# A batched matrix product: one of eight output groups stored in six strided transfers

## The chip, the cores and the metric

The kernel runs on one core of a Trainium2 chip. The metric is the device time of one execution in microseconds, as the median of several runs.

## The reference

```python
batch, dim_i, dim_j, dim_k = 32, 256, 512, 384
x: (32, 256, 512) float32,  y: (32, 512, 384) float32

def reference(x, y):
    return np.einsum('bij,bjk->bik', x, y).astype(np.float32)
```

Thirty-two independent products of a 256 x 512 matrix with a 512 x 384 matrix, read and written in float32: 16.8 MB of x, 25.2 MB of y and 12.6 MB of output.

## The kernel before

**Tiling.** The 32 batches are worked in N = 8 groups of Q = 4. In a group each batch has PQ = 32 of the 128 partitions. For x and for the output a partition holds R = 8 consecutive rows of its batch, for y T = 16 consecutive rows. So in memory each partition's share of a group is one contiguous run: 16 KB of x, 24 KB of y, 12 KB of output. The output run falls into two halves of 6 KB, one for each half `e` (NE = 2; H = 4 rows of 384 floats).

**Engines.** SyncE (SP) issues all transfers. x and y have two buffers each, and a group's loads are issued when the casts of the group two before it have freed them. GpSimd (POOL) casts x and y to float16 (`round_x` at line 126, `round_y` at line 136). VectorE (DVE) transposes x in 32 x 32 blocks (line 156). TensorE (PE) multiplies with four 32-row tiles, one for each batch of the group (line 217). ScalarE (ACT) and DVE copy the sums from PSUM to `o_sb` (both at line 165): of 16 blocks of a half, DVE takes the last five and ACT the other eleven. `o_sb` has room for all eight groups, so a store never has to make room for later work.

**SP's order.** SP's queue is written out by hand. After the loads (lines 69 and 73) it waits until the first chunk of group 5's second half has been multiplied (all copies of groups 0 to 4 are done then) and stores groups 0 to 4 (JOINED = 5) in one transfer. It waits for the same point in the last group, 7, and stores groups 5 and 6 in one transfer. Then it waits for ACT and DVE to finish and stores group 7. At the end (line 111) it waits until every transfer has added 16 to the semaphore `s_out`. All three stores go through `store` (the transfer is line 96), each with all 128 partitions as its outermost dimension. The transfers of SP's queue are worked off by the core's 16 DMA engines.

Of the kernel before, what the change touches and what calls it, by code (L numbers as in the profile page):

```python
# [11 lines left out]
Q = 4  # L12
NE = 2
STEP = 4
STRAIGHT = 2
JOINED = 5
# [3 lines left out]
def kernel(  # L20
# [11 lines left out]
    PQ = P // Q  # L32
    R = I // PQ
    H = R // NE
    T = J // PQ
    TW = T // 2
    N = B // Q
    NC = T // STEP

    def sbuf(name, shape, dtype):  # L40
        return nc.alloc_sbuf_tensor(name, shape, dtype).ap()
# [3 lines left out]
    o_sb = sbuf("o_sb", [P, N, NE, H, K], F32)  # L45
# [16 lines left out]
    s_out = nc.alloc_semaphore("s_out")  # L62
# [25 lines left out]
    def chunk_done(n, e, a):  # L88
        return (n * NE + e) * MARKS + (a + 1 if a < NC - 1 else MARKS)

    sp = nc.sync

    def store(first, last):
        groups = out[first * Q : last * Q].rearrange("(n g) (s f) k -> (g s) n f k", g=Q, s=PQ)
        src = o_sb[:, first:last].rearrange("p n e h k -> p n (e h) k")
        sp.dma_start(out=groups, in_=src).then_inc(s_out, 16)

    for n in range(2, N):
# [3 lines left out]
        load_y(n)  # L102
    sp.wait_ge(s_pe, chunk_done(JOINED, NE - 1, 0))
    store(0, JOINED)
    sp.wait_ge(s_pe, chunk_done(N - 1, NE - 1, 0))
    store(JOINED, N - 1)
    sp.wait_ge(s_act, NE)
    sp.wait_ge(s_dve, NE)
    store(N - 1, N)
    sp.sem_inc(s_sp, 1)  # L110
    sp.wait_op(s_out, 16 * 3, "sem-ge").then_inc(s_out, -16 * 3)

# [116 lines left out]
    with te.Fori(0, N):  # L231
        with te.Fori(0, NE) as e:
            take(s_act)
            take(s_dve)
            for t in range(T):
# [3 lines left out]
                for g in range(Q):  # L239
                    s = slice(g * PQ, (g + 1) * PQ)  # L240
# [40 lines left out]
```

## Time and profile before

| | |
|---|---|
| time, median of 3 runs | 131.95 us (131.85 to 132.28) |
| the profiled execution, its own time | 132.13 us |
| its span, first to last instruction | 130.8 us |
| DMA engines busy (SP's queue) | 98.1% |
| DVE, ACT, POOL, PE busy | 63%, 64%, 57%, 47% |
| moved | 41.94 MB read, 12.58 MB written, 417 GB/s over the span |
| transfers issued | 16 loads, 3 stores |

The page of the profile gives busy times in microseconds and as a share of the span. Its slices are forty equal parts of the span; each digit is a busy share in tenths. The lines on transfers give for each group of issues the number, the size of one, and the time from issue to landing. A row of the windows view gives a stretch of the span, its length, the busy time of each engine with the number of instructions, the granted TensorE clock, the DMA share and the GB/s. In the waits of SP's queue a row names the waiting line, what it waited for, the total, the number of waits and the longest.

### The profile page before, as it was taken

To read this page: it belongs to the slowest core of one execution; us is meant where nothing else is said; L and a number is where in the kernel's file an instruction comes from. 1 tells how busy PE (TensorE), PEld (TensorE's weight loads), DVE (VectorE), ACT (ScalarE), POOL (GpSimd) and SP (SyncE) were. 2 spreads that over 40 slices of the span, in tenths; PEclk is the share of its full clock that TensorE was granted. 3 is DMA by queue.
4 is the path that set the end of the run, shared out by engine and by line. 5 is a ranking of instruction groups with operands and counts; after the bars stand their busy time and mean duration, and the time that the engine had idled before them with its cause. 6 is when DMAs were issued, how large, how long until landed. Compare 5 with 4: busy or idle time off the path is not lost. (4 is left out here: it accounts for less than half of the span.)

```text
span 130.8 us, 3199 instructions
## 1 busy us (share of the span) xinstructions
PE 61.4 (47%) x1024; PEld 46.7 (36%) x1024; DVE 82.7 (63%) x144; ACT 84.1 (64%) x178; POOL 74.2 (57%) x42
## 2 busy tenths in 40 slices
PE   0000009910992589089329905980975499100000
PEld 0000009800991566046129604970953236000000
DVE  0000036899379999985997997599999957920000
ACT  0400000599659989993998899399999957994000
POOL 0006991199929965992899459758973970000000
PEclk9999999995589689977986985599599959965555
DMA  5999999999999999999999999999999999999995
GB/s 120 451 396 441 421 431 451 443 408 428 451 413 421 438 443 401 436 436 443 423 458 398 443 408 466 398 418 436 463 398 408 427 438 425 436 428 421 425 440 248
DMA packets 3379, 54.55 MB, mean 417 GB/s; under 512 B 304, under 2 KB 304, under 8 KB 304
## 3 DMA queue, kind: packets, MB, share of 16 engines
q1 hardware_dynamic: 3376, 54.53, 98.1%
q14 instruction: 3, 0.02, 0.0%
HBM read 41.94 MB, written 12.58 MB: 417 GB/s over the span
## 5 line engine op out<-in xcount | busy, mean ns | idle before, releaser
L165 ACT COPY o_sb<-o_ps (+1 forms) x176 | 82.6, 469 | 31.7 <-PE o_ps L217 29.6
L217 PE MATMUL o_ps<-y_r,xt_sb 32*128 32x384 f16 x1024 | 61.4, 384 | 50.4 <-PEq L214 49.5
L217 PEld LDWEIGHTS o_ps<-y_r,xt_sb 32*128 32x128 f16 x1024 | 46.7, 107 | 64.6 <-issue 56.8
L156 DVE STREAM_TRANSPOSE xt_sb<-x_r 128x256 f32<-128x256 f32 x64 | 38.1, 626 | 30.9 <-POOL x_r L126 18.4
L136 POOL CAST y_r<-y_sb 128x1536 f16<-128x1536 f32 (+1 forms) x22 | 44.3, 2049 | 15.8 <-DMA y_sb<-in_y_dram 15.3
L165 DVE COPY o_sb<-o_ps 32x384 f32 (+1 forms) x80 | 44.6, 557 | 1.6
L126 POOL CAST x_r<-x_sb 128x2048 f16<-128x2048 f32 x16 | 30.2, 1893 | 16.8 <-DVE o_sb L165 12.1
L202 ACT ACT_TABLE_LOAD x1 | 1.3, 1283 | 3.4 <-PEq L78 3.4
L265 POOL MEMSET const-float32-0.0<- 128x1 f32 x1 | 0.1, 98 | 0.2 <-issue 0.2
L202 ACT COPY spare<-const-float32-0.0 1x1 f32<-1x1 f32 x1 | 0.2, 190 | 0.0
L265 POOL MEMSET const-bfloat16-1.0<- 128x1 bf16 x1 | 0.1, 101 | 0.0
L265 POOL MEMSET const-uint8-127<- 128x1 uint8 x1 | 0.1, 101 | 0.0
L265 POOL MEMSET const-float32-1.0<- 128x1 f32 x1 | 0.1, 98 | 0.0
## 6 DMA issues: line engine op xcount, KB each, us to landing
y_sb<-in_y_dram SPq DMA_DIRECT2D x8, 3072.0 KB, 16.8
x_sb<-in_x_dram SPq DMA_DIRECT2D x8, 2048.0 KB, 17.0
out_dram<-o_sb SPq DMA_DIRECT2D x1, 7680.0 KB, 33.9
out_dram<-o_sb SPq DMA_DIRECT2D x1, 3072.0 KB, 17.3
out_dram<-o_sb SPq DMA_DIRECT2D x1, 1536.0 KB, 11.5
```

Of the source, the lines that this page charges most:

```text
L126: po.tensor_copy(x_r[:, e], x_sb[n % 2][:, e * H : (e + 1) * H]).then_inc(s_cast, 1)
L136: ins = po.tensor_copy(y_r[:, s], y_sb[n % 2][:, s])
L156: v.transpose(xt_w[:, w], words[:, e, w]).then_inc(s_xt, 1)
L165: ins = copy(o_sb[g * PQ : (g + 1) * PQ, n, e, h], o_ps[h * PQ : (h + 1) * PQ, e * Q + g, :K],)
L202: a_.copy(spare, nc.const_aps.tensor(0.0, [1, 1], F32))
L217: return te.add_instruction(mybir.InstMatmult(name=nc.get_next_instruction_name(), start_tensor_calc=start, stop_tensor_calc=stop, tile_si ...
L265: nc = _bacc.Bacc("TRN2", target_bir_lowering=False, num_devices=1)
```

## The change

Groups 5 and 6 are no longer stored in one transfer. Group 5 is stored by itself in the old form. Group 6 goes out in six transfers, called rows here for the partitions that they take:

| transfer | partitions | number | bytes of each |
|---|---|---|---|
| 1 | 0, 2, 4, ... | 64 | 12 KB |
| 2 | 1, 5, 9, ... | 32 | 12 KB |
| 3 | 3, 11, 19, ... | 16 | 12 KB |
| 4 | 7, 15, 23, ... | 16 | the first 6 KB |
| 5 | 7, 23, 39, ... | 8 | the second 6 KB |
| 6 | 15, 31, 47, ... | 8 | the second 6 KB |

Together they write each byte of group 6 once. The store of group 7 stays as it was and is issued after them. The last wait counts nine stores in place of three.

```diff
+    def store_cut(n):
+        dst = out[n * Q : (n + 1) * Q].rearrange("g (s f) k -> (g s) f k", s=PQ)
+
+        def rows(first, step, e0, e1):
+            sp.dma_start(
+                out=dst[first::step, e0 * H : e1 * H],
+                in_=o_sb[first::step, n, e0:e1].rearrange("p e h k -> p (e h) k"),
+            ).then_inc(s_out, 16)
+
+        rows(0, 2, 0, NE)
+        rows(1, 4, 0, NE)
+        rows(3, 8, 0, NE)
+        rows(7, 8, 0, 1)
+        rows(7, 16, 1, NE)
+        rows(15, 16, 1, NE)
...
     sp.wait_ge(s_pe, chunk_done(N - 1, NE - 1, 0))
-    store(JOINED, N - 1)
+    store(JOINED, N - 2)
+    store_cut(N - 2)
     sp.wait_ge(s_act, NE)
     sp.wait_ge(s_dve, NE)
     store(N - 1, N)
     sp.sem_inc(s_sp, 1)
-    sp.wait_op(s_out, 16 * 3, "sem-ge").then_inc(s_out, -16 * 3)
+    sp.wait_op(s_out, 16 * 9, "sem-ge").then_inc(s_out, -16 * 9)
```

## The prediction

> **What bounds the kernel now.** I read the page's shares and slices first, then its transfers, then SP's queue, then the last microseconds in narrow windows.
>
> ```profile
> span 130.8 us, 3199 instructions
> PE 61.4 (47%) x1024; PEld 46.7 (36%) x1024; DVE 82.7 (63%) x144; ACT 84.1 (64%) x178; POOL 74.2 (57%) x42
> DMA  5999999999999999999999999999999999999995
> DMA packets 3379, 54.55 MB, mean 417 GB/s; under 512 B 304, under 2 KB 304, under 8 KB 304
> q1 hardware_dynamic: 3376, 54.53, 98.1%
> ```
>
> No compute engine is busy for two thirds of the span, while the sixteen DMA engines are busy for 98.1% of it. The time is the bytes over the rate of the DMA engines, and what is left to win lies at the two ends. The packets fit the shapes: 3376 less 304 small ones is 3072, which is 24 transfers (eight of y, eight of x, eight groups of output) of 128 rows, one packet a row; 304 is 19 issued transfers by 16 engines, so each engine closes each transfer with one small packet.
>
> ```profile
> y_sb<-in_y_dram SPq DMA_DIRECT2D x8, 3072.0 KB, 16.8
> x_sb<-in_x_dram SPq DMA_DIRECT2D x8, 2048.0 KB, 17.0
> out_dram<-o_sb SPq DMA_DIRECT2D x1, 7680.0 KB, 33.9
> out_dram<-o_sb SPq DMA_DIRECT2D x1, 3072.0 KB, 17.3
> out_dram<-o_sb SPq DMA_DIRECT2D x1, 1536.0 KB, 11.5
> ```
>
> Every transfer of this trace takes all 128 rows: the smallest, the 1536 KB of group 7, is 128 rows of 12 KB, eight for each engine. Nothing here shows a transfer of 64, 32, 16 or 8 rows, or rows with a step between them. That is the unknown of this change.
>
> SP's queue and its waits say when the stores are issued:
>
> ```profile
> L96 SPq DMA_DIRECT2D out_dram<-o_sb x3: 345/390/403, 85.9 to 119.3; - x3
> 109.82 0.39 SPq L96 DMA_DIRECT2D out_dram<-o_sb  x1
> 119.27 0.34 SPq L96 DMA_DIRECT2D out_dram<-o_sb  x1
> SPq L108 <- DVE o_sb L165: 5.0, 1, 5.0
> SPq L96 <- ACT o_sb L165: 4.0, 1, 4.0
> SPq L111 <- SPq L111: 11.1, 1, 11.1
> ```
>
> The store of groups 5 and 6 goes out at 109.82 us and that of group 7 at 119.27 us, after SP has waited 5.0 us for DVE and 4.0 us for ACT. Adding the landing times above, the three stores land at 119.8, 127.1 and 130.8 us: each is issued while an older one is still running, so the engines never lack work. The chain of waits ends with SP standing 11.1 us at line 111 for the last bytes.
>
> Now the end itself. In these windows a packet is counted where it starts; the last two columns are the DMA share and GB/s.
>
> ```profile
> 112.00:118.00 6.00, 0.00 (x0) 0.00 (x0) 3.09 (x6) 5.83 (x14) 0.00 (x0) 0.77 1.01 430
> 118.00:126.00 8.00, 0.00 (x0) 0.00 (x0) 0.00 (x0) 1.22 (x3) 0.00 (x0) 0.50 1.00 427
> 126.00:129.00 3.00, 0.00 (x0) 0.00 (x0) 0.00 (x0) 0.00 (x0) 0.00 (x0) 0.50 1.02 434
> 129.45:129.50 0.05, 0.00 (x0) 0.00 (x0) 0.00 (x0) 0.00 (x0) 0.00 (x0) 0.50 1.14 482
> 129.50:129.84 0.34, 0.00 (x0) 0.00 (x0) 0.00 (x0) 0.00 (x0) 0.00 (x0) 0.50 0.01 0
> 129.84:129.86 0.02, 0.00 (x0) 0.00 (x0) 0.00 (x0) 0.00 (x0) 0.00 (x0) 0.50 1.47 615
> 129.86:130.80 0.94, 0.00 (x0) 0.00 (x0) 0.00 (x0) 0.00 (x0) 0.00 (x0) 0.50 0.00 0
> ```
>
> 430 GB/s over 16 engines is 26.9 GB/s for one, so a 12,288-byte row takes 0.457 us. 615 GB/s in 0.02 us are 12.3 KB: one single packet starts at 129.85 us, and by its share (1.47 x 0.02 x 16) it runs 0.47 us, to 130.32. The 0.48 us from there to the span's end are its landing and the release of SP. Before it no packet starts for 0.34 us, and the 482 GB/s in the 0.05 us ahead are two packets, which end at about 129.94. So **one engine is late by 0.38 us, alone**; only a change to what that engine does, or to all the others by more than 0.38 us, moves the end.
>
> **The change, part by part.** The profiled execution took 132.13 us, 1.33 more than its span and 0.18 more than the median of 131.95; I work out differences on the span and put them on the median.
>
> *Bytes.* Group 6 is still 128 rows of 12 KB: nothing is added or removed. Group 5 alone keeps the old form.
>
> *Issues.* At 109.82 us SP now issues seven transfers in place of one. Six more by at most 0.403 us are 2.4 us, done by about 112.6. SP then waits for DVE and ACT until 119.27 in any case, so 6.6 us of cover hide them; what is queued behind is only the store of group 7. The data are not late either: the engines come to group 6 only when the 119.8 us store and group 5 (eight rows, 8 x 0.457 = 3.7 us) are done, after 122 us. Cost 0; without cover it would be up to 2.4 us.
>
> *Closing packets.* Six more transfers mean up to six more small packets on each engine. The window from 126 to 129 us holds the seam between two stores and shows 434 GB/s, against 427 before it: the seam costs nothing that can be seen. A hundredth of its 3 us, 0.03, is the most that such a row could hide. I take 0.01 each, +0.06 in all, with 0 and 0.18 as ends.
>
> *The shifted half rows.* A half row is 0.457 / 2 = 0.23 us. The transfer of sixteen half rows gives each engine one, if rows are dealt evenly; the two transfers of eight rows can occupy only eight engines each. If these are the same eight, eight engines do a half row more than before and eight a half row less. If the late engine is among those relieved, it ends at 130.32 - 0.23 = 130.09, but one of the two at 129.94 may then be loaded and end at 130.17, so the end comes 0.15 to 0.23 us earlier. If the late engine is loaded, the end comes 0.23 us later. If the two transfers fall on different eights, nothing moves. No view numbers the engines, so the trace cannot say which. I take the relief, -0.16, because a relief changes the end in the way that the single late packet allows, and keep +0.23 as the other end.
>
> [...]
>
> *The price of a row in the new transfers.* This is the term with far ends. Below, a row with a step costs what every row of this trace costs, 0.457 us, loads and stores alike: the three windows from 112 to 129 us lie between 427 and 434 GB/s. Above, if two engines meet on the same path at the memory's side and take turns, each row costs twice that: eight rows by 0.457 us are +3.66 us. A gain is hardly there, since the engines already run at one rate whatever they carry; I allow 0.1 us. The value I take is 0, by the nearest row, the 128-row store of the same 12 KB rows. Sum: -0.16 + 0.06 + 0 + 0 = **-0.10 us**, 131.85 us, with 131.6 to 132.3 as this case's own range (-0.23 - 0.1 to +0.23 + 0.18).
>
> **The rivals.** *The small transfers pile up (slower).* The transfers of sixteen and eight rows touch rows 3, 11, 19 and so on, or 7, 23, 39: few rows, far apart, at once on all engines that take part. If they meet pairwise there, one full row (0.457), one half row (0.23) and, on eight engines, two half rows (0.46) take twice their time: +1.14 us at most; engines that are out of step by some tenths of a microsecond (above, 0.38 between the last and those before it) meet less, so I take +0.9: 132.85 us, from 132.4 to 133.3. It decides as soon as an engine loses more than its 0.38 us of slack plus the 0.4 us that can be told from no change. For it: no such transfer is in the trace, and the row rate is the same for loads and stores, as if one common path were full. Against it: the rate holds at 1.00 to 1.02 through all seams.
>
> [...]
>
> *All six pile up (much slower).* If each engine takes its rows as a run of neighbours in the stepped list, engine 0 has rows 0, 2, 4, 6, and if engines some distance apart then meet in step on all eight of their rows, the full +3.66 us is due, less the offset at each meeting: +2 to +3.7, at the middle 134.8 us. For and against as above; against it also that the steps of 2 and 4 spread rows over the whole height, as 128 rows do.
>
> *Another instruction fetch falls on the late engine (slightly slower).* The trace holds three, all around 100 to 106 us:
>
> ```profile
> q14 instruction: 3, 0.02, 0.0%
> ```
>
> 0.02 MB by three is some 7 to 8 KB, 0.3 us at 26.9 GB/s. SP's program grows by six transfers; if one more fetch results and hits the late engine, the end moves by +0.3, or +0.5 with what it interrupts: 132.35 us. On another engine the 0.38 us hide it.
>
> **How the numbers follow.** About 0.3%, 0.4 us, is what a measurement of this kernel can tell from no change. I give the even row price 0.44, the pile-up of the small transfers 0.27, that of all six 0.23, and the fetch 0.06. The rows as such favour the first; the unseen shape of all six transfers keeps the two pile-ups together at one half. Faster by over 0.4 us needs more than the 0.23 us of a half row, so only an unforeseen gain in the first case: 0.07. Within: the rest of the first case, 0.37, and a third of the fetch, 0.02: 0.39. Slower: 0.27 + 0.23 + 0.04 = 0.54. Slower holds more chance than the likeliest single case, and the range says so: from 131.6, the first case's low end, through the small pile-up to 134.8, the middle of the large one. It leaves out half of that last case and little at the bottom.
>
> **What would show it.** Right: in the profile after, the windows from 119 us on stay at 427 to 434 GB/s to 129 us, the last packet starts between 129.6 and 129.9, seven issues stand at 109.8 to 112.6 us and SP still waits for ACT until 119.3. Wrong by a pile-up: with bytes unchanged, the window that holds group 6's rows (from 122 to 126 us) drops to between 215 and 380 GB/s, or the DMA share there stays at 1.0 while GB/s fall; the span's end then moves past 131.5. If only the small transfers pay, the fall lies in the last third of that stretch. If the half rows fall on other engines than assumed, the gap before the last packet is 0.6 us or stays at 0.34. An end before 130.4 us would show a gain that I have no step for.

## The result and the profile after

| | before | after |
|---|---|---|
| median | 131.95 us (131.85 to 132.28, 8 runs) | 132.32 us (132.20 to 132.55, 8 runs) |
| ratio | | 1.0028, 95% interval 1.0019 to 1.0037 |
| profiled execution, span | 132.13 us, 130.8 us | 132.20 us, 130.8 us |

The change costs 0.37 us. That is just under the 0.4 us that I had called a difference one can tell, but with eight runs on each side the interval is clear of one. The forecast was 0.10 us in the other direction. The profiled execution after is the fastest of its eight, and that of before lies 0.18 us above its median, so the two spans are equal; what differs is the order of the last microseconds.

From the page of the changed kernel, then SP's issues, a line's view and SP's waits:

```profile
span 130.8 us, 3205 instructions
DMA  4999999999999999999999999999999999999995
DMA packets 3475, 54.55 MB, mean 417 GB/s; under 512 B 384, under 2 KB 384, under 8 KB 416
q1 hardware_dynamic: 3472, 54.53, 98.1%
q14 instruction: 3, 0.02, 0.0%
...
L99 SPq DMA_DIRECT2D out_dram<-o_sb x6: 932/1070/1100, 110.6 to 116.1; - x6
L114 SPq DMA_DIRECT2D out_dram<-o_sb x3: 333/350/408, 86.5 to 119.6; - x3
...
110.20 0.35 SPq L114 DMA_DIRECT2D out_dram<-o_sb  x1
110.59 6.50 SPq L99 DMA_DIRECT2D out_dram<-o_sb  x6
119.55 0.33 SPq L114 DMA_DIRECT2D out_dram<-o_sb  x1
...
SPq L130 <- SPq L130: 10.9, 1, 10.9
SPq L114 <- ACT o_sb L184: 2.4, 1, 2.4
```

The kernel is bound as before, by 98.1% busy DMA engines. The 32 half rows are the 416 - 384 packets between 512 B and 8 KB. The small packets that close transfers rise from 304 to 384: the 80 more are sixteen for each of four transfers and eight for each of the two of eight rows, so each of these two ran on eight engines. SP needs a median of 1.07 us for each of the six issues (L99), not the 0.33 to 0.41 of a whole store (L114); all six are out at 117.1 us, and SP still waits 2.4 us for ACT. So the issues stay hidden, with about a quarter of the 9 us of cover left.

The windows of the end, changed kernel (the columns are as in the prediction; a packet counts where it starts):

```profile
122.00:125.00 3.00, 0.00 (x0) 0.00 (x0) 0.00 (x0) 0.00 (x0) 0.00 (x0) 0.50 0.99 420
125.00:126.60 1.60, 0.00 (x0) 0.00 (x0) 0.00 (x0) 0.00 (x0) 0.00 (x0) 0.50 1.02 411
126.60:129.00 2.40, 0.00 (x0) 0.00 (x0) 0.00 (x0) 0.00 (x0) 0.00 (x0) 0.50 1.02 435
129.00:129.50 0.50, 0.00 (x0) 0.00 (x0) 0.00 (x0) 0.00 (x0) 0.00 (x0) 0.50 0.41 172
129.50:130.00 0.50, 0.00 (x0) 0.00 (x0) 0.00 (x0) 0.00 (x0) 0.00 (x0) 0.50 0.29 123
129.99:130.01 0.02, 0.00 (x0) 0.00 (x0) 0.00 (x0) 0.00 (x0) 0.00 (x0) 0.50 1.51 647
```

and the same two half microseconds of the kernel before:

```profile
129.00:129.50 0.50, 0.00 (x0) 0.00 (x0) 0.00 (x0) 0.00 (x0) 0.00 (x0) 0.50 0.75 320
129.50:130.00 0.50, 0.00 (x0) 0.00 (x0) 0.00 (x0) 0.00 (x0) 0.00 (x0) 0.50 0.07 25
```

GB/s times the stretch, divided by 12.3 KB, counts packets. Before, 13 start between 129.0 and 129.5 us and one after it, at 129.85. After, it is seven, then five, then one at 130.00. So before, one engine alone starts its last packet after 129.5 us; after, five do (the fifth packet before 130.0 is the last engine's last but one), and the last packet starts 0.15 us later.

The packet records of the two traces (start, length and bytes of every packet) say which engines these are. The packets of one engine stand end to end there, so that sixteen chains can be followed back from the end. After the change, eight chains hold three half rows of group 6 and eight hold one: the two transfers of eight rows did run on the same eight engines. The six engines that end last all have three, and the last engine with one ends 0.79 us before the end. Three of the 32 half rows took 0.38 to 0.60 us in place of 0.23, and one of them, of 0.38 us, is on the engine that ends last.

The windows agree: 122 to 125 us hold the transfers of 64 and 32 rows at full rate; 125 to 126.6, with the transfers of sixteen and eight rows, carry 411 GB/s at a share of 1.02, that is 403 for each full share against 424 to 426 in the rows around it.

### The profile page after: what moved, and what is told of

It reads as the page before. It is cut to its first block, busy times and chain, and to the rows that moved or that the text cites. A ratio compares the mean times of both kernels' runs of the same rounds, so it can differ in the third digit from the quotient of the medians.

```text
span 130.8 us, 3205 instructions
## 1 busy us (share of the span) xinstructions
PE 65.4 (50%) x1024; PEld 54.0 (41%) x1024; DVE 82.5 (63%) x144; ACT 84.1 (64%) x178; POOL 74.0 (57%) x42
## 3 DMA queue, kind: packets, MB, share of 16 engines
q1 hardware_dynamic: 3472, 54.53, 98.1%
## 5 line engine op out<-in xcount | busy, mean ns | idle before, releaser
L236 PE MATMUL o_ps<-y_r,xt_sb 32*128 32x384 f16 x1024 | 65.4, 409 | 46.7 <-PEq L233 43.3
L236 PEld LDWEIGHTS o_ps<-y_r,xt_sb 32*128 32x128 f16 x1024 | 54.0, 114 | 57.7 <-issue 51.7
```

What stands on the lines that cost most here:

```text
L236: return te.add_instruction(mybir.InstMatmult(name=nc.get_next_instruction_name(), start_tensor_calc=start, stop_tensor_calc=stop, tile_si ...
```

## The experiments

All are the changed kernel with other transfers for group 6, except e6; each was timed in five rounds beside the kernel before on the same chip. One half row is 6 KB, 0.23 us.

| run | group 6 | median, us | before, us | ratio (95% interval) |
|---|---|---|---|---|
| e1_no_shift | steps 2, 4, 8, 8; no shift | 132.19 | 131.88 | 1.0017 (0.9997 to 1.0038) |
| e2_six_even | six transfers, no shift | 132.26 | 131.88 | 1.0016 (0.9997 to 1.0036) |
| e3_double_shift | steps 2, 4, 8; twice the shift | 132.64 | 131.88 | 1.0041 (1.0020 to 1.0063) |
| e5_by_sevens | half rows by sevens | 132.50 | 131.88 | 1.0029 (1.0007 to 1.0052) |
| e4_two_blocks | rows 0 to 63, 64 to 127 | 135.38 | 131.97 | 1.0249 (1.0223 to 1.0274) |
| e6_eight_whole | whole; eight stores in all | 132.01 | 131.97 | 1.0005 (0.9992 to 1.0019) |
| e7_step_two | two transfers, step 2 | 132.07 | 131.97 | 1.0005 (0.9994 to 1.0017) |
| e8_step_eight | eight transfers, step 8 | 134.21 | 131.97 | 1.0172 (1.0154 to 1.0190) |
| e9_step_four | four transfers, step 4 | 132.07 | 131.99 | 1.0002 (0.9989 to 1.0016) |
| e10_shift_clean | the shift, no step of 8 | 132.38 | 131.99 | 1.0024 (1.0009 to 1.0039) |
| e11_shift_twice | twice that shift | 132.54 | 131.99 | 1.0037 (1.0024 to 1.0051) |
| e12_change_again | the change | 132.43 | 131.99 | 1.0030 (1.0017 to 1.0042) |
| e13_load_two | extra on two engines | 132.20 | 131.92 | 1.0019 (1.0002 to 1.0035) |
| e14_load_four | extra on four engines | 132.42 | 131.92 | 1.0042 (1.0025 to 1.0058) |

**Is it the shift?** I began with theory 1, that the two transfers of eight rows load the engine that is late anyway, against the number of transfers (theory 2) and the steps (theory 3).

```diff
 # e1_no_shift
-        rows(7, 8, 0, 1)
-        rows(7, 16, 1, NE)
-        rows(15, 16, 1, NE)
+        rows(7, 8, 0, NE)
```

> Group 6 by steps of 2, 4 and 8, the last sixteen rows whole in one transfer: four transfers, each engine its eight rows, no half row shifted. Theory 1 (the half rows fall on the engine that is late anyway): the 0.37 us are gone, 131.9 to 132.1 us, and the last packet starts alone, over 0.3 us after the one before it, as in the kernel before. Theory 2 (many small transfers and their closing packets cost): two thirds of the loss stay, 132.2 us. Theory 3 (stepped rows meet on a path of the memory): all of it stays, 132.3 us, since the stepped rows are all here.

Measured 1.0017: theory 1 does not get back all it had claimed. The median lies 0.31 us above before, but the interval reaches one, so this run alone does not show a loss.

```diff
 # e2_six_even: the second half rows as two transfers of 16 rows by 3 KB
-        rows(7, 16, 1, NE)
-        rows(15, 16, 1, NE)
+        part(7, 8, 4, 6)
+        part(7, 8, 6, 8)
```

> Six transfers again, but all of 64, 32 or 16 rows: the last sixteen rows as 6 KB, 3 KB and 3 KB, so that every engine has the same bytes. Theory 1: 131.95 to 132.1 us (only six seams more). Theory 2: as the change or worse, 132.3 us, since the number of transfers and of closing packets is at least that of the change. Theory 3: 132.3 us.

1.0016, as e1: two transfers more than e1 add nothing that can be seen. That speaks against theory 2 already.

```diff
 # e3_double_shift
-        rows(7, 8, 0, 1)
-        rows(7, 16, 1, NE)
-        rows(15, 16, 1, NE)
+        rows(7, 16, 0, NE)
+        rows(15, 16, 0, NE)
```

> The last sixteen rows whole in two transfers of eight rows: five transfers, twice the shift (12 KB instead of 6 KB more on eight engines and less on the other eight). Theory 1: another half row, 0.23 us, on top of the change: 132.5 to 132.65 us. Theory 2: one transfer less and no half rows: 132.1 to 132.25 us. Theory 3: as the change, 132.3 us.

1.0041, the most of the four, with fewer transfers than the change, and the median of 132.64 us is what theory 1 had; theories 2 and 3 had 132.1 to 132.3. It is no clean dose of the shift, though: in its packet records two rows on the last engine took 0.94 and 0.98 us in place of 0.46.

```diff
 # e5_by_sevens
-        rows(7, 16, 1, NE)
-        rows(15, 16, 1, NE)
+        some(7, 63, 8, 1, NE)
+        some(63, 119, 8, 1, NE)
+        some(119, 128, 8, 1, NE)
```

> The sixteen second half rows in two transfers of seven rows and one of two in place of two of eight. If the engines are taken from the lowest number up, engines 0 to 6 get one half row more than an even share would give, 0 and 1 two more where the last pair falls, and 7 to 15 one less. Theory 1 with the late engine being number 7: the late engine is now relieved, 131.75 to 131.95 us, and the lone last packet of the profile is gone or 0.2 us earlier. Theory 1 with the late engine among 0 to 6: 132.3 us or more. Theory 2: one transfer more than the change, 132.4 us.

1.0029, no better than the change. In the order of engines that the expectation supposes, an eighth engine that is the late one would have been relieved, which speaks against that guess. But no view numbers the engines, so that the order is not shown, and in that order the run also puts two half rows more on two engines: it does not settle which engine it is.

**Do the steps cost?** Theory P supposes a path at the on-chip memory (SBUF) that engines share and take turns on; theory S supposes a price for each transfer. Which rows would meet on such a path no run before these shows. As estimates, theory P has for e4 up to the 3.66 us of the prediction, eight rows at twice 0.457 us, and for e8 1.2 us, four times the 0.3 us by which e1, with two transfers of sixteen rows, lay above before. e7 stores group 6 in two transfers of 64 rows, the even and the odd ones.

```diff
 # e4_two_blocks
-        rows(0, 2, 0, NE)
...
+        some(0, 64, 1, 0, NE)
+        some(64, 128, 1, 0, NE)
```

> Group 6 in two transfers of neighbouring rows, 0 to 63 and 64 to 127. [...] Theory S (each transfer more costs some 0.07 us): two more than in the kernel before, +0.1 to +0.15 us.

```diff
 # e6_eight_whole, against the kernel before
-    store(0, JOINED)
+    for n in range(JOINED):
+        store(n, n + 1)
...
-    store(JOINED, N - 1)
+    for n in range(JOINED, N - 1):
+        store(n, n + 1)
```

> The kernel before with each group stored by itself, eight stores of all 128 rows instead of three: five more transfers and closing packets for each engine, no step and no half row. Theory P: no change, within 0.1 us of before. Theory S: five times 0.07 us, +0.35 us.

```diff
 # e7_step_two
+        rows(0, 2, 0, NE)
+        rows(1, 2, 0, NE)
 # e8_step_eight, in its place
+        for i in range(8): rows(i, 8, 0, NE)
```

> [...] Theory P as the changed kernel shows it (no loss in its transfers of 64 and 32 rows, a loss in those of 16 and 8): within 0.1 us of before. Theory P where the engines meet in step: +1.5 us or more. Theory S: two more transfers than in the kernel before, +0.1 to +0.15 us.

> Group 6 in eight transfers of 16 rows, eight partitions apart, each engine one row of each. [...] Theory S: eight more transfers than in the kernel before (with group 5 by itself), +0.5 to +0.6 us, with GB/s lower by no more than a twentieth.

The windows of e4 first, then e8, then e7:

```profile
122.00:126.00 4.00, 0.00 (x0) 0.00 (x0) 0.00 (x0) 0.00 (x0) 0.00 (x0) 0.50 1.05 359
126.00:129.00 3.00, 0.00 (x0) 0.00 (x0) 0.00 (x0) 0.00 (x0) 0.00 (x0) 0.50 0.96 266
...
122.00:123.00 1.00, 0.00 (x0) 0.00 (x0) 0.00 (x0) 0.00 (x0) 0.00 (x0) 0.50 1.08 430
123.00:129.00 6.00, 0.00 (x0) 0.00 (x0) 0.00 (x0) 0.00 (x0) 0.00 (x0) 0.50 0.99 330
...
122.00:125.00 3.00, 0.00 (x0) 0.00 (x0) 0.00 (x0) 0.00 (x0) 0.00 (x0) 0.50 0.98 418
125.00:126.60 1.60, 0.00 (x0) 0.00 (x0) 0.00 (x0) 0.00 (x0) 0.00 (x0) 0.50 1.07 453
```

The engines stay busy to a share of 0.96 and 0.99 while the bytes fall to 266 and 330 GB/s: packets take longer. In the packet records about half of the 128 rows of group 6 are slow, up to 2.07 us in e4 and 1.21 us in e8 in place of 0.46; in e7 none is. Two blocks of neighbouring rows lose 3.4 us and eight transfers of sixteen rows 2.2 us, while the even and odd rows lose nothing that can be seen. Five whole transfers more cost nothing that can be seen either (e6), where theory S had +0.35 us. Theory S is out. Of theory P's estimates 3.66 us is near the measured 3.4, and 1.2 us for e8 is too little. The runs change the partitions and the addresses in the output together, so they show neither that there is a shared path nor that it lies at SBUF; that stays a supposition. What they show is which patterns lose: 135.38 and 134.21 against 132.07 us.

```diff
 # e9_step_four
+        for i in range(4): rows(i, 4, 0, NE)
```

> Group 6 in four transfers of 32 rows, four partitions apart: as many transfers as in the run with the last sixteen rows whole, and as many stepped rows, but none of sixteen or eight rows. [...] If the loss is that of any four stepped transfers: +0.3 us.

1.0002: four stepped transfers, as many as e1, lose nothing that can be seen if they have 32 rows each. So the price lies in the transfers with rows eight and sixteen apart. e1 has two of those; a fourth of e8's 2.2 us would be 0.56 us, and e1 shows 0.2 to 0.3 us of it, not separated from zero. In e1's packet records two of these 32 rows are slow, 0.81 and 0.94 us in place of 0.46; what these two cost the run does not show.

**The shift without the steps of eight.**

```diff
 # e10_shift_clean; cols(first, stop, a, b): every 4th row, columns a to b of 8 (1.5 KB each)
+        for i in (1, 2, 3): rows(i, 4, 0, NE)
+        cols(0, 128, 0, 6)
+        for i in (0, 32, 64, 96): cols(i, i + 32, 6, 8)
 # e11_shift_twice: the columns are cut at 4 instead of 6
```

> The change's shift without its steps of eight and sixteen: three transfers of 32 rows, four partitions apart, whole; of the remaining 32 rows the first 9 KB in one transfer, the last 3 KB in four transfers of eight rows each, four partitions apart. If eight rows run on the same eight engines, these get 6 KB more than an even share and the other eight 6 KB less, as in the change. Theory 1 (the late engine is one of the loaded eight): +0.2 to +0.3 us against before. If the side of the late engine makes no difference: within 0.1 us of before. If the late engine is relieved: -0.1 us.

> The same with 6 KB in each of the four transfers of eight rows: twice the shift. Theory 1: a further 0.2 us, +0.4 to +0.55 us against before. If the late engine is relieved: the end is set by the loaded engines, 0 to +0.2 us.

> The change itself once more, beside the three others: +0.37 us as before, +0.25 to +0.45. If loss by steps of eight and by the shift add up, the run with four transfers and no shift (+0.3 us) and the clean shift give this number or more together.

e10's end:

```profile
125.00:126.60 1.60, 0.00 (x0) 0.00 (x0) 0.00 (x0) 0.00 (x0) 0.00 (x0) 0.50 0.97 405
126.60:129.00 2.40, 0.00 (x0) 0.00 (x0) 0.00 (x0) 0.00 (x0) 0.00 (x0) 0.50 1.04 440
129.50:130.00 0.50, 0.00 (x0) 0.00 (x0) 0.00 (x0) 0.00 (x0) 0.00 (x0) 0.50 0.47 197
130.00:130.50 0.50, 0.00 (x0) 0.00 (x0) 0.00 (x0) 0.00 (x0) 0.00 (x0) 0.50 0.18 74
130.50:131.00 0.50, 0.00 (x0) 0.00 (x0) 0.00 (x0) 0.00 (x0) 0.00 (x0) 0.50 0.06 25
```

Bytes for each full share are 418 and 423 GB/s, so packets are hardly slowed here, although four of the transfers have only eight rows; yet four packets start after 130.0 us. In the packet records no packet of group 6 is slow, and the last engine is again one of the eight with the extra bytes; the other eight end 1.0 us and more before it. The shift alone makes 1.0024, nearly all of the change's 1.0030 beside it, and twice the shift 1.0037. It has the sign of theory 1; that twice the shift costs more is likely, but the two intervals overlap. The two causes need not add up (e1 and e10 together would be 1.0041), since the end is that of the last of sixteen engines and not a sum; the intervals are too wide to say more.

**Where the shift falls.** If the late engine is among those loaded, loading others should be harmless.

```diff
 # e13_load_two; CUT is 512 bytes before the end of a row
+        rows(1, 2, 0, NE)
+        cols(0, 128, 2, 0, CUT)
+        cols(0, 124, 2, CUT, W)
+        cols(124, 128, 2, CUT, W)
 # e14_load_four
+        cols(0, 128, 1, 0, CUT)
+        cols(0, 124, 1, CUT, W)
+        cols(124, 128, 1, CUT, W)
```

> Group 6 in two transfers of 64 rows (odd rows whole, even rows without their last 512 bytes), and these last 512 bytes in a transfer of 62 rows and one of two. 62 rows divide evenly over no more than two engines, so these two get some 0.6 to 0.8 us more than an even share and the other fourteen 0.08 us less. Theory 1 (what counts is whether the late engine is among the loaded ones; it is not one of the lowest two): 131.85 to 132.05 us, nothing lost against before although the shift is larger than in any run until now. Rival (any shift of this size costs, wherever it falls): 132.3 us or more. Were the late engine one of these two: 132.6 us.

> All 128 rows of group 6 without their last 512 bytes in one transfer, and the last 512 bytes in a transfer of 124 rows and one of four, which divide evenly over no more than four engines: these get some 0.55 to 0.75 us more and the other twelve 0.15 us less. Theory 1 with the late engine outside the lowest four: 131.8 to 132.05 us. With the late engine among them: 132.5 us or more, as rival (any shift of this size costs).

The lowest two and the lowest four are an assumption on the order of the engines, which no view shows; how many took part is shown. Of e13's 340 small packets 336 are sixteen for each of 21 transfers; the four that are left fit two engines for each of the two pieces. Of e14's 328, 320 are sixteen for each of 20 transfers; the eight that are left fit four engines for each piece.

e13 came out at 132.20 us, between two of the forecasts, and its profiled execution ends with a lone packet once more:

```profile
129.00:129.50 0.50, 0.00 (x0) 0.00 (x0) 0.00 (x0) 0.00 (x0) 0.00 (x0) 0.50 0.64 270
129.50:130.00 0.50, 0.00 (x0) 0.00 (x0) 0.00 (x0) 0.00 (x0) 0.00 (x0) 0.50 0.06 25
```

The estimated 0.6 to 0.8 us, about three times the half row's 0.23 us, put on two engines, costs no more than the half row on eight (1.0019 against 1.0024, intervals overlapping), so where it falls may matter. But it is not free. The packet records say why: in both runs the engine that ends last is one that carries the pieces of 512 bytes. It ends 0.42 us (e13) and 0.78 us (e14) after the last engine that carries none. So a loaded engine became the last one, and e13 and e14 do not show by their times which engine was the late one.

The records show it in another way. In each trace where it could be followed, one engine alone works off a run of slow rows, 0.47 to 0.55 us in place of 0.46, between 107 and 112 us. In the kernel before, that engine has the lone last packet. In the changed kernel and in e10 it is one of the eight that get the extra bytes; in e13 and e14 it is not among the two and four that do. If it is the same engine in all of them, the change loaded the late engine. Even so, it ends 0.13 us before the last in the changed kernel's trace and 0.43 us before it in e10's (in the former its chain meets another's once, so it may also be the last): any of the loaded engines can be the one that ends last.

## Why the prediction was wrong

*The bound, and the lone last packet:* right on the bound. The DMA engines set the time, and both runs end with a single packet. But the 0.38 us by which one engine was late were read from one execution: with nothing shifted, the last engine ends 0.40 us after the next in e7's trace, 0.11 in e6's and 0.08 in e9's. A relief of that engine could not have been worth 0.16 us in every execution.

*Issues:* mis-sized and harmless. I took 0.40 us each from whole transfers; these take 1.07. They end at 117.1 us instead of 112.6, and 2.4 us of cover remain.

*Closing packets:* nothing speaks against +0.06 us: a closing packet takes 9 ns in the packet records, and five transfers more in e6 give 1.0005 (0.9992 to 1.0019).

*The shifted half rows:* this step failed. I worked out -0.16 if the late engine is relieved and +0.23 if it is loaded, found no view that decides, and took the relief. The loss is on the other side. In the profile after, the last packet starts at 130.00 us instead of 129.85, five engines start theirs after 129.5 us where there was one, and all five carry three half rows; every engine with one half row ends at least 0.79 us before the end. The shift without the steps of eight costs 0.24% (e10). That both transfers take the same eight engines was an assumption when the step was written; the trace shows it, with eight engines of three half rows and eight of one.

*The price of a row:* this step failed too, though less is known of its size. It was set to 0 by the nearest row; the windows from 112 us on, named there for loads and stores alike, hold stores only (the last packet of a load starts at 99.7 us). The 0 was right for the transfers of 64 and 32 rows (e7, e9) and wrong for those with rows eight apart (e8, +2.2 us for eight of them). What two of them cost inside the change is, by e1, between nothing and 0.3 us. In the profiled execution the slow half row of 0.38 us in place of 0.23 sits on the last engine, so that end is made by both steps.

*The rivals:* "the small transfers pile up" named a loss that exists, but its +0.9 us was too much. I had doubled every row of these transfers on the estimate that engines meet pairwise; no run shows such a meeting, and three of the 32 half rows were slow in the change and two of the 32 rows in e1, which lost 0.2 to 0.3 us. "All six pile up" is out: e7 (1.0005) and e9 (1.0002). A loss of the size that it had does occur, 3.4 us, where 64 neighbouring rows go out together (e4). The fetch did not come: the page after has three as well.

The case's own range, with the +0.23 in it, reaches to 131.95 + 0.41 = 132.36 us, which was written as 132.3; the measured 132.32 is at that end. The error was to choose a sign where no row gave one, and to call the choice the likeliest.

## What to carry to other kernels

In this kernel, whose DMA engines are busy for 98.1% of the span, the time was that of the last engine. A half row more on eight engines and less on the other eight cost 0.24% (e10), with a loaded engine last; it could have helped only if the engine that ends last had been relieved and none of the loaded ones had overtaken it. Transfers could be cut along partitions without a loss that can be seen in pieces of 32 rows four apart (e9, 1.0002) or 64 rows two apart (e7, 1.0005); pieces of 64 neighbours (e4, 1.0249) or of 16 rows eight apart (e8, 1.0172) slowed about half of their rows. The number of transfers as such cost nothing that can be seen while they were issued well ahead (e6, 1.0005).

## What the runs showed of the hardware

In the changed kernel SP takes 0.93 to 1.10 us to issue each part of group 6 and 0.33 to 0.41 us for each whole store; the step is not the reason by itself, since the unstepped halves of e4 took 0.83 to 0.96 us each and the three unstepped pieces of e14 2.50 us together. Five more closed transfers on a full queue cost nothing measurable (1.0005). A transfer of eight rows ran on eight engines (384 small packets in place of 304). A store of 64 neighbouring rows in place of 128 brings the rate from 430 to 266 GB/s while the engines stay 96% busy, so the busy share alone would have shown nothing: the bytes for each busy share do. One engine alone had a run of rows of 0.47 to 0.55 us in place of 0.46 between 107 and 112 us; in the kernel before it is the engine that ended last.
